# Second mixer's projections: who rounds the weights, and how many PSUM buffers the products have

## Chip, cores and metric

One core of a Trainium2 chip. The metric is the device time of one execution in microseconds (us); before and after are compared by medians of several executions. The profile is one execution taken by the hardware profiler, with times from its first instruction.

## What is computed

A two-layer backbone over 512 latent and 256 context tokens of width 1024. Layer 1 mixes tokens with a bidirectional chunkwise mLSTM; its projections are the stretch in question:

```
p = (t @ w_in).astype(float32)          # t: normalised, modulated tokens (768 x 1024), w_in: 1024 x 3104
q = heads(p[..., :512], 64) * 64 ** -0.5
k = heads(p[..., 512:1024], 64)
v = heads(p[..., 1024:2048], 128)
o = p[..., 2048:3072]                   # later: sigmoid(o), latent tokens only
g = p[..., 3072:3104] + b_gates         # input and forget gates, both directions
```

After it come the mLSTM itself, its output projection, and the mixture of experts of layer 1, whose weights (32 experts) are streamed from HBM.

## The kernel before

Engines: PE = TensorE, ACT = ScalarE, DVE = VectorE, POOL = GpSimd, SP = SyncE, which here issues the loads from HBM.

**Split products.** Matmuls run on a reduced-precision float type (F32R). So each operand is split into a rounded part (hi) and the rest (lo = x - hi), and each product is three matmuls: hi·hi, hi·lo, lo·hi. `Net.split` (L303) does one split: hi on ACT (L306) if no engine is given for it, else with a `tensor_scalar` on that engine (L308); lo with a `tensor_sub` (L309), on POOL for weights. The inner `split` of `ml_in` (L1663) does this for a weight tile of 1024 x 256 in two halves of 128 x 1024 values each; its `eng` is the engine of hi, and None (ACT) by default.

**`ml_in` (L1637).** In a first part, in an order written out by hand (`manual_schedule`, L1709 to 1732), the tokens are transposed and modulated (`norm_T`) for k = 0 to 7, each followed by `chans` (L1688): the products of that k for the gates (PSUM tile psg) and for the first 256 columns of q (psq). Then a loop over i = 0 to 11 takes 256 columns of w_in at a time (i = 0 is done already): i = 1 the second half of q, 2 and 3 k, 4 to 7 v, 8 to 11 o. Each turn loads its weights (L1660, called L(i) below), splits them (split(i)), forms products by `chan` (L1672, 24 matmuls of 512 columns) or by token tile with `toks` (L1680, 24 matmuls of 256 columns), and ACT empties each finished PSUM tile into SBUF (L1769, 1771, 1776, 1782, 1789). A turn of v has six token tiles, a turn of o four.

Between them, turns 1 to 8 do two quarters of the layer's modulation on DVE (`ada_vec`, L194: two loads of 1 MB at L168, then 16 DVE instructions, L202 and L204). Its `finish` comes a turn later, behind the products: tiny matmuls (L210), additions (L214, L218), in some turns a transpose (L227) and a store (L230). `tokens` (L1846) at i = 3 and `ml_queries` (L1879) at i = 9 add some PE and DVE work.

**Buffers.** The pool `ws` has three buffers of 1 MB for L(i) and the ada loads together. `wk` (L1647) has four for each part, so the halves of two turns. `pa` (L1648) has two PSUM tiles of two banks each; a product uses half of one at most. `pb` takes the other four banks. Outside the manual part a scheduler orders each engine's instructions at compile time, by priorities and a cost model, and gives out buffers as it goes; so the order on an engine need not be that of the program, but it is fixed when the kernel runs, and each engine, and SP, works its list in order.

Of the kernel before, what the change touches and what calls it, by code (L numbers as in the profile page):

```python
# [6 lines left out]
F32 = mybir.dt.float32  # L7
# [7 lines left out]
PSUM = bass.MemoryType.PSUM  # L15
ET = mybir.EngineType

P = 128
# [84 lines left out]
class Net:  # L103
# [1533 lines left out]
    def ml_in(self, x, xcp, wsp):  # L1637

        tc, nc, A = self.tc, self.nc, self.A
        V = nc.vector  # L1640
        W = A["l1_ml_w_in"]
        with ExitStack() as st:
            def pool(name, bufs=1, **kw):
                return st.enter_context(tc.tile_pool(name=name, bufs=bufs, **kw))

            hp = pool("h1", side="right")
            wk = pool("i1", 4, side="right")  # L1647
            pa = pool("pa1", 2, space=PSUM)  # L1648
            pb = pool("pb1", 2, space=PSUM)
            hcp = tc.tile_pool(name="h1c", bufs=1, side="right")  # L1650
            hc = hcp.__enter__()
            hs = [[q.tile([P, KD, n], F32R, name=f"h{m}{n}") for m in ("hi", "lo")] for q, n in ((hc, CTX), (hp, SEQ))]
# [5 lines left out]
            def load(c0, n):  # L1658
                w = wsp.tile([P, KD, n], F32, name="ws")
                nc.sync.dma_start(w, W[:, c0:c0 + n].rearrange("(k p) f -> p k f", p=P))  # L1660
                return w

            def split(w, n=256, pool=wk, name="", eng=None, halves=(0, 1)):  # L1663
                parts = []
                for a in halves:
                    hi = pool.tile([P, 4, n], F32R, name=f"{name}whi")
                    lo = pool.tile([P, 4, n], F32R, name=f"{name}wlo")
                    self.split(hi, lo, w[:, 4 * a:4 * a + 4, :], nc.gpsimd, eng)
                    parts.append((hi, lo))
                return parts  # L1670

            def chan(ps, parts, c, t0, t1):  # L1672

                for k in range(KD):
                    (hi, lo), (xh, xl) = parts[k // 4], hk(k, t0, t1)
                    for j, (w, h) in enumerate(((hi, xh), (hi, xl), (lo, xh))):
                        nc.tensor.matmul(ps, w[:, k % 4, c * P:(c + 1) * P], h,
                                         start=k == 0 and j == 0, stop=k == KD - 1 and j == 2)

            def toks(ps, parts, t):  # L1680

                for k in range(KD):
                    (hi, lo), (xh, xl) = parts[k // 4], hk(k, t * P, (t + 1) * P)
                    for j, (w, h) in enumerate(((hi, xh), (hi, xl), (lo, xh))):
                        nc.tensor.matmul(ps, h, w[:, k % 4, :],  # L1685
                                         start=k == 0 and j == 0, stop=k == KD - 1 and j == 2)

            def chans(out, k):  # L1688

                for ps, parts, c, t0, t1 in out:  # L1690
                    (hi, lo), (xh, xl) = parts[k // 4], hk(k, t0, t1)
                    for j, (w, h) in enumerate(((hi, xh), (hi, xl), (lo, xh))):
                        nc.tensor.matmul(ps, w[:, k % 4, c * P:(c + 1) * P], h,
                                         start=k == 0 and j == 0, stop=k == KD - 1 and j == 2)
# [6 lines left out]
            wq0 = load(0, 256)  # L1701
# [6 lines left out]
            wgp = wsp.tile([P, KD, 4, 32], F32, name="ws")  # L1708
            with tc.tile_pool(name="n2", bufs=2, side="right") as wp, tc.manual_schedule(engines={ET.PE, ET.DVE, ET.Activation, ET.Pool}):  # L1709
                nc.gpsimd.memset(wgp, 0.0)  # L1710
                for a in (0, 16):
                    nc.gpsimd.tensor_scalar(wgp[:, :, :, a:a + 8], wg0.rearrange("p k (j h) -> p k j h", h=8),
                                            1.0, 0.0, op0=OP.mult, op1=OP.add)
                parts = split(wgp.rearrange("p k j h -> p k (j h)"), P, wp, "g", nc.gpsimd)
                parts0 = split(wq0, 256, wp, "q", nc.gpsimd)
                turn, modulate = self.norm_T(1, x, self.rs, hs,
                                             lambda: pb.tile([P, 1024], F32, name="pg"), wn)
                psg = pa.tile([P, 1024], F32, name="pa")
                psq = pa.tile([P, 1024], F32, name="pa")
                first = [(psg[:, 512:1024], parts, 0, CTX, NTOK), (psg[:, 256:512], parts, 0, 0, CTX),  # L1720
                         (psq[:, 0:512], parts0, 0, CTX, NTOK), (psq[:, 512:1024], parts0, 1, CTX, NTOK)]
                turn(0)
                turn(1)
                w = load(256, 256)
                parts1 = []
                for k in range(KD):
                    modulate(k)
                    if k + 2 < KD:
                        turn(k + 2)
                    chans(first, k)  # L1730
                    if k in (2, 5):
                        parts1 += split(w, halves=(k // 3,))
# [16 lines left out]
            ps = psg  # L1749
            for q in range(4):  # L1750
                dst = (self.li, self.lf)[q % 2][32 * (q // 2):32 * (q // 2) + 32, :]
                nc.scalar.activation(dst, ps[32 * q:32 * q + 32, 256:1024], AF.Identity, bias=bg[32 * q:32 * q + 32, :])
            tokens = self.ml_gates(sp, gp, pb)

            ada = []
            for i in range(12):
                parts = parts1 if i == 1 else split(load(256 * i, 256)) if i else None
                last, ada = ada, []
                if 1 <= i <= 8:
                    ada = [self.ada_vec(1, 6 + 2 * i + j, wsp, pb, sp, m=1) for j in range(2)]  # L1760
                if i == 0:
                    pass
                elif i < 4:
                    for c in range(2):
                        blk = 2 * (i % 2) + c
                        ps = pa.tile([P, 1024], F32, name="pa")[:, 0:512]
                        chan(ps, parts, c, CTX, NTOK)
                        if i < 2:
                            nc.scalar.activation(self.qT[:, blk, :], ps, AF.Copy, scale=0.125)  # L1769
                        else:  # L1770
                            nc.scalar.activation(self.kT[:, blk, :], ps, AF.Copy)
                    if i >= 2:
                        for t in range(2):
                            ps = pa.tile([P, 1024], F32, name="pa")[:, 0:256]
                            toks(ps, parts, t)
                            nc.scalar.activation(self.kc[:, t, 256 * (i - 2):256 * (i - 1)], ps, AF.Copy)
                elif i < 8:
                    for t in range(NT0):
                        ps = pa.tile([P, 1024], F32, name="pa")[:, 0:256]
                        toks(ps, parts, t)  # L1780
                        h = 2 * (i - 4)
                        nc.scalar.activation(self.v1[:, t, h:h + 2, 0:128],  # L1782
                                             ps.rearrange("p (h e) -> p h e", e=128), AF.Copy)
                else:
                    for t in range(4):
                        ps = pa.tile([P, 1024], F32, name="pa")[:, 0:256]
                        toks(ps, parts, 2 + t)
                        c = slice(256 * (i - 8), 256 * (i - 7))
                        nc.scalar.activation(self.og[:, t, c], ps, AF.Sigmoid)
                if i == 3:  # L1790
                    tokens()
                    gates.__exit__(None, None, None)
                if i == 7:
                    hcp.__exit__(None, None, None)
                if i == 9:
                    self.ml_queries(store.enter_context(tc.tile_pool(name="queries", bufs=1)), pb)
                for f in last:
                    f()
# [371 lines left out]
```

## Time and profile before

| | |
|---|---|
| median of 3 runs | 1930.48 us (1927.62 to 1940.3) |
| the profiled execution | 1943.99 us, span 1942.0 us |
| busy in the span | PE 93%, DVE 49%, ACT 28%, POOL 20% |
| mean granted clock of TensorE | 0.959 |
| `ml_in` from the last products of its first part to the last product | about 1059 to 1263 us |

An answer of the timeline has one line for a group of instructions that follow each other on an engine: start, length of the group, engine, line, operation, output<-input, number; in brackets the idle time in front and what ended it. A length that covers several instructions contains their waits in between. For SP, the start of a line is when the load is issued; it lands later, and the first reader of the data shows when.

### The profile page before, as it was taken

The page shows a single profiled execution, that of the slowest core. Times are in us where ns is not written, and L with a number is a line of the kernel's source. Part 1 is how long each engine was busy: PE and PEld are TensorE (multiplying, and loading weights), DVE is VectorE, ACT ScalarE, POOL GpSimd, SP SyncE. Part 2 cuts the span into 40 slices and gives each one's busy share as a digit, 9 for nine tenths or more (in the row PEclk, how much of TensorE's full clock was granted, in tenths as well). Part 3 has the DMA queues.
Part 4 walks back from the last instruction along what each step waited for, and adds up shares of the span by engine and source line. Part 5 has one row for each costly group of instructions (what it writes and reads, how often), then busy time and mean ns, then how long its engine had stood idle before and what let it go on. Part 6 is the DMA issues. An engine that isn't in the chain of part 4 may idle for free. (4 is left out here: it accounts for less than half of the span.)

```text
span 1942.0 us, 26118 instructions
## 1 busy us (share of the span) xinstructions
PE 1799.0 (93%) x10181; PEld 1009.0 (52%) x10181; DVE 959.3 (49%) x1879; ACT 542.7 (28%) x1007; POOL 387.7 (20%) x300
## 2 busy tenths in 40 slices
PE   7999988897999999999987998999978999999996
PEld 5777775683333333333336898976743333333332
DVE  5577767465454454444455743155552333233334
ACT  5367776222111101111115421145321111111112
POOL 3443311501101000101015242121211111110101
PEclk9999989898999999999998998999988999999998
DMA  9645432547999789999932544200869999999993
GB/s 326 186 142 163 152 109 76 188 152 311 420 419 397 278 326 409 389 403 389 400 117 76 176 139 155 85 1 17 311 257 400 421 421 420 421 422 421 421 420 135
DMA packets 158244, 527.75 MB, mean 272 GB/s; under 512 B 15132, under 2 KB 92194, under 8 KB 109988
## 3 DMA queue, kind: packets, MB, share of 16 engines
q1 hardware_dynamic: 151348, 497.09, 66.5%
q0 software_dynamic: 6768, 28.93, 3.8%
q8 instruction: 82, 1.34, 0.3%
q14 instruction: 46, 0.38, 0.1%
HBM read 518.59 MB, written 7.39 MB: 271 GB/s over the span
## 5 line engine op out<-in xcount | busy, mean ns | idle before, releaser
L1215 DVE TENSOR_TENSOR xl<-xl,ps 128x512 f32<-128x512 f32 x252 | 172.4, 687 | 335.6 <-PE ps L1213 335.6
L1213 PEld LDWEIGHTS ps<-yh,oht 128*128 128x128 f32 x310 | 58.5, 189 | 248.8 <-DVE xl L1215 129.0
L1213 PE MATMUL ps<-yh,oht 128*128 128x512 f32 x310 | 154.1, 497 | 8.9 <-DVEq L1356 6.1
L1200 POOL DMA_INDIRECT xg<-h_rows,idx x32 | 36.7, 1146 | 628.8 <-DVE slot L1185 263.1
L1277 PE MATMUL pd<-wring,hT 128*64 128x512 f32 (+1 forms) x616 | 152.4, 611 | 3.0 <-ACT hT L1269 2.6
L1252 PE MATMUL pu<-wring,xT 128*64 128x512 f32 (+1 forms) x576 | 154.1, 606 | 0.0
L309 POOL TENSOR_TENSOR wlo<-ws,whi 128x1024 fp32r<-128x1024 f32 x41 | 114.8, 2809 | 120.9 <-ACT whi L306 119.4
L1252 PE MATMUL pg<-wring,xT 128*64 128x512 f32 (+1 forms) x576 | 136.9, 601 | 0.0
L1240 POOL TENSOR_TENSOR yl<-yw,yh 128x512 fp32r<-128x512 f32 x60 | 76.6, 1277 | 255.5 <-ACT yh L1239 255.5
L1213 PE MATMUL ps<-yl,oht 128*128 128x512 f32 x310 | 123.5, 398 | 0.0
L1259 ACT ACTIVATE sg<-pg 128x512 f32<-128x512 f32 x32 | 19.1, 597 | 367.6 <-PE pg L1252 367.6
L1685 PE MATMUL pa<-whi,hhi 128*128 128x256 f32 x352 | 104.3, 296 | 9.1 <-ACT v L1782 9.0
L1239 ACT ACTIVATE yh<-yw 128x512 fp32r<-128x512 f32 x64 | 40.3, 630 | 251.7 <-DVE yw L1236 127.9
L1231 DVE SCALAR_TENSOR_TENSOR yw<-pd,slotr,gt2b 128x512 f32<-128x512 f32 x62 | 46.5, 751 | 118.9 <-PE pd L1277 118.9
L1685 PE MATMUL pa<-whi,hlo 128*128 128x256 f32 x352 | 103.3, 293 | 0.0
L1685 PE MATMUL pa<-wlo,hhi 128*128 128x256 f32 x352 | 102.9, 292 | 0.0
L1252 PE MATMUL pu<-yt,xT 128*64 128x512 f32 (+1 forms) x408 | 101.7, 605 | 0.0
L1208 ACT ACTIVATE xT<-tr 128x512 f32<-128x512 f32 x64 | 35.1, 596 | 221.0 <-PE tr L1207 221.0
L1277 PE MATMUL pd<-yt,hT 128*64 128x512 f32 (+1 forms) x376 | 87.6, 599 | 1.5 <-ACT hT L1269 1.0
L1252 PE MATMUL pg<-yt,xT 128*64 128x512 f32 (+1 forms) x400 | 84.7, 599 | 0.0
L1215 DVE TENSOR_TENSOR xc<-xc,ps 128x512 f32<-128x512 f32 x64 | 43.7, 687 | 82.1 <-PE ps L1213 82.0
L1277 PEld LDWEIGHTS pd<-wring,hT 128*64 128x64 f32 (+1 forms) x616 | 44.3, 133 | 75.7 <-issue 69.6
(627 smaller groups left out, 3727.9 us busy)
## 6 DMA issues: line engine op xcount, KB each, us to landing
wring<-in_l_moe_w_gate_dram SPq DMA_DIRECT2D x62, 1024.0 KB
wring<-in_l_moe_w_up_dram SPq DMA_DIRECT2D x61, 1024.0 KB
wring<-in_l_moe_w_down_dram SPq DMA_DIRECT2D x59, 1024.0 KB
yt<-in_l_moe_w_up_dram SPq DMA_DIRECT2D x41, 1024.0 KB
ws<-in_l_ada_w_dram SPq DMA_DIRECT2D x40, 1024.0 KB
yt<-in_l_moe_w_gate_dram SPq DMA_DIRECT2D x39, 1024.0 KB
yt<-in_l_moe_w_down_dram SPq DMA_DIRECT2D x35, 1024.0 KB
ws<-in_l_moe_w_gate_dram SPq DMA_DIRECT2D x24, 1024.0 KB
```

Source lines behind the costliest of these rows:

```text
L309: eng_lo.tensor_sub(lo, x, hi.bitcast(F32))
L1200: nc.gpsimd.indirect_dma_start(out=xg, out_offset=None, in_=hd, in_offset=bass.IndirectOffsetOnAxis(ap=idx[:, 0:1], axis=0))
L1208: nc.scalar.activation(xT[:, 4 * h:4 * h + 4, :], pt[:, :, 0:n], AF.Copy)
L1213: nc.tensor.matmul(ps, lhsT, y, start=i == 0, stop=i == len(ys) - 1)
L1215: V.tensor_add(xs, xs, ps)
L1231: V.scalar_tensor_tensor(y[k], ps, r[:, 1:2], g[:, 0, :], op0=OP.mult, op1=OP.mult)
L1239: nc.scalar.activation(yh, y, AF.Copy)
L1240: eng.tensor_sub(yl, y, yh.bitcast(F32))
L1252: nc.tensor.matmul(ps[a:a + w, :], xT[:, 4 * h + j, a:a + w], pieces[n, e[i], h][:, j, :], start=h == 0 and j == 0, stop=h == 1 and j == 3)
L1259: nc.scalar.activation(s, pg, AF.Silu)
L1277: nc.tensor.matmul(pd[a:a + w, :], hT[:, 2 * h + j, a:a + w], ring.down(2 * p + i, h, j, c), start=h == 0 and j == 0, stop=h == 1 and j == 1)
L1685: nc.tensor.matmul(ps, h, w[:, k % 4, :], start=k == 0 and j == 0, stop=k == KD - 1 and j == 2)
```

## The change

The inner `split` rounds on GpSimd by default, so ACT has no weight split left in `ml_in`; POOL does hi and lo one after the other. The two large PSUM tiles of the first part move into a pool of their own, `pa0`, which is closed before the loop; the loop gets a pool of four single-bank tiles in the same four banks.

```
-            pa = pool("pa1", 2, space=PSUM)
             pb = pool("pb1", 2, space=PSUM)
+            pa0 = tc.tile_pool(name="pa0", bufs=2, space=PSUM)
+            pa = pa0.__enter__()
...
-            def split(w, n=256, pool=wk, name="", eng=None, halves=(0, 1)):
+            def split(w, n=256, pool=wk, name="", eng=nc.gpsimd, halves=(0, 1)):
...
-                parts = split(wgp.rearrange("p k j h -> p k (j h)"), P, wp, "g", nc.gpsimd)
-                parts0 = split(wq0, 256, wp, "q", nc.gpsimd)
+                parts = split(wgp.rearrange("p k j h -> p k (j h)"), P, wp, "g")
+                parts0 = split(wq0, 256, wp, "q")
...
             tokens = self.ml_gates(sp, gp, pb)
+            pa0.__exit__(None, None, None)
+            pa = pool("pa1", 4, space=PSUM)
...
-                        ps = pa.tile([P, 1024], F32, name="pa")[:, 0:512]
+                        ps = pa.tile([P, 512], F32, name="pa")
...
-                            ps = pa.tile([P, 1024], F32, name="pa")[:, 0:256]
+                            ps = pa.tile([P, 512], F32, name="pa")[:, 0:256]
```

The last edit is made at all three places where `toks` gets its PSUM tile (L1774, 1779, 1786).

## Rows read from the trace of the kernel before

**Rows 1.** Busy us of PE, PEld, DVE, ACT, POOL (instructions); clock, DMA share, GB/s.
```profile
1116.00:1263.00 147.00, 133.91 (x1024) 130.17 (x1023) 50.34 (x118) 29.64 (x54) 43.10 (x14) 0.93 0.40 127
...
1500.00:1600.00 100.00, 98.31 (x458) 35.40 (x456) 31.39 (x62) 12.59 (x26) 14.35 (x11) 1.00 1.01 421
```

**Rows 2.** What SP waited for, whole span: total us, times, longest.
```profile
SPq L93 <- DVE keys L2008: 119.6, 1, 119.6
```

**Rows 3.** Timeline of PE, turns i = 5, 7, 8 and 9.
```profile
1134.68 0.36 PE L1685 MATMUL pa<-whi,hhi 128*128 128x256 f32 x1
1141.71 0.39 PE L1685 MATMUL pa<-whi,hhi 128*128 128x256 f32 x1 [3.92 <-ACT v L1782]
1146.18 0.28 PE L1685 MATMUL pa<-whi,hhi 128*128 128x256 f32 x1
...
1149.06 0.28 PE L1685 MATMUL pa<-whi,hhi 128*128 128x256 f32 x1
...
1176.77 0.36 PE L1685 MATMUL pa<-whi,hhi 128*128 128x256 f32 x1
1190.21 0.28 PE L1685 MATMUL pa<-whi,hhi 128*128 128x256 f32 x1
...
1202.53 0.36 PE L1685 MATMUL pa<-whi,hhi 128*128 128x256 f32 x1
1209.75 0.41 PE L1685 MATMUL pa<-whi,hhi 128*128 128x256 f32 x1
...
1219.57 0.36 PE L1685 MATMUL pa<-whi,hhi 128*128 128x256 f32 x1
```

**Rows 4.** Timeline of ACT, the hi halves of split(4), split(6) and split(8).
```profile
1102.55 2.01 ACT L306 ACTIVATE whi<-ws 128x1024 fp32r<-128x1024 f32 x2 [5.46 <-DMA ws<-in_l_ml_w_in_dram]
...
1139.38 2.00 ACT L306 ACTIVATE whi<-ws 128x1024 fp32r<-128x1024 f32 x2 [7.80 <-DMA ws<-in_l_ml_w_in_dram]
...
1182.66 2.00 ACT L306 ACTIVATE whi<-ws 128x1024 fp32r<-128x1024 f32 x2 [8.99 <-DMA ws<-in_l_ml_w_in_dram]
```

**Rows 5.** Timeline of SP, the loads into `ws`.
```profile
1090.00 0.99 SPq L168 DMA_DIRECT2D ws<-in_l_ada_w_dram  x2
1097.15 0.37 SPq L1660 DMA_DIRECT2D ws<-in_l_ml_w_in_dram  x1
...
1128.08 1.01 SPq L168 DMA_DIRECT2D ws<-in_l_ada_w_dram  x2
...
1169.83 0.99 SPq L168 DMA_DIRECT2D ws<-in_l_ada_w_dram  x2
```

**Rows 6.** Timeline of POOL, the lo halves of split(5) and split(7).
```profile
1120.36 7.69 POOL L309 TENSOR_TENSOR wlo<-ws,whi 128x1024 fp32r<-128x1024 f32 x2 [10.32 <-ACT whi L306]
...
1159.53 10.27 POOL L309 TENSOR_TENSOR wlo<-ws,whi 128x1024 fp32r<-128x1024 f32 x2 [12.71 <-ACT whi L306]
```

**Rows 7.** Durations of the split's instructions: ns min/median/max, first and last start.
```profile
L306 ACT ACTIVATE whi<-ws x22: 1040/1058/1115, 1037.0 to 1231.3; 128x1024 fp32r<-128x1024 f32 x22
L309 POOL TENSOR_TENSOR wlo<-ws,whi x22: 2332/2400/7920, 1040.2 to 1233.3; 128x1024 fp32r<-128x1024 f32 x22
...
L308 POOL TENSOR_SCALAR whi<-ws x19: 1041/1054/2485, 22.4 to 293.0; 128x1024 fp32r<-128x1024 f32 x19
```

**Rows 8.** Timeline of ACT and PE from the first part into the loop.
```profile
1059.09 1.06 ACT L306 ACTIVATE whi<-ws 128x1024 fp32r<-128x1024 f32 x1 [2.93 <-DMA ws<-in_l_ml_w_in_dram]
1060.05 0.40 ACT L306 ACTIVATE hhi<-hf 128x256 fp32r<-128x256 f32 x1
...
1063.50 0.89 ACT L1752 ACTIVATE li<-pa,bg 32x768 f32<-32x768 f32 x1 [2.10 <-PE pa L1693]
...
1065.56 1.08 ACT L1748 ACTIVATE qT<-pa 128x512 f32<-128x512 f32 x2 [0.27 <-PE pa L1693]
...
1062.90 0.39 PE L1693 MATMUL pa<-hlo,gwhi 128*128 128x256 f32 x1 [2.02 <-DVE hlo L309]
...
1066.70 0.79 PE L1677 MATMUL pa<-hhi,whi 128*128 128x512 f32 x1 [1.17 <-ACT qT L1748]
```

More of the change, by code (lines that the diff above doesn't have):

```diff
@@ L1778, in ml_in @@
                     for t in range(NT0):
-                        ps = pa.tile([P, 1024], F32, name="pa")[:, 0:256]
+                        ps = pa.tile([P, 512], F32, name="pa")[:, 0:256]
                         toks(ps, parts, t)
@@ L1785, in ml_in @@
                     for t in range(4):
-                        ps = pa.tile([P, 1024], F32, name="pa")[:, 0:256]
+                        ps = pa.tile([P, 512], F32, name="pa")[:, 0:256]
                         toks(ps, parts, 2 + t)
```

## The prediction, made before the changed kernel ran

> **What bounds the kernel now.** I read the busy time in windows first. In the loop of `ml_in`, PE is busy for 133.9 of 147 us, while ACT, POOL and DVE are busy for 29.6, 43.1 and 50.3 [rows 1]. So PE is the bound, and the mean granted clock of 0.93 says that some of the rest is time after a pause, at the lower of the two levels. What can be won here is PE's pauses with what follows them, nothing else. The next question is whether a gain here reaches the end. The first expert load of layer 1 waits 119.6 us on SP for the last work of the attention that follows `ml_in` [rows 2], and once it runs the DMA engines are full (share 1.01 and 421 GB/s from 1500 to 1600 us [rows 1]). The stream is long and begins when the attention ends: what `ml_in` saves moves the whole stream forward, one for one.
>
> Then the timeline of PE. One undisturbed token tile takes 2.88 us (1146.18 to 1149.06). At the start of turn 5 two tiles take 11.50 us instead of 5.76, and at the start of turn 7 13.44 (1176.77 to 1190.21); the row at 1141.71 names the releaser, an emptying copy on ACT [rows 3]. The timeline of ACT shows why it was late: in ACT's list the hi copies of a later turn's weights stand in front of the emptying copies of a tile that is done, and they wait 7.8 and 9.0 us for a load to land [rows 4]. With two PSUM tiles PE can go on for one tile, then it stands. After the pause the second tile still takes 4.47 us (1141.71 to 1146.18), which is the lower clock.
>
> **The change, part by part.**
>
> *ACT loses the weight splits.* Twenty-two copies of 1.06 us [rows 7] leave ACT; their 23 us are worth nothing as such, as ACT has time. What counts is that an emptying copy no longer stands behind a DMA wait. That takes away 11.50 - 5.76 = 5.7 us in turn 5 and 13.44 - 5.76 = 7.7 us in turn 7. In turn 8 one tile takes 7.22 us (1202.53 to 1209.75 [rows 3]), 4.3 too many; no ACT copy of weights ended that pause, so I credit between 0 and 4.3.
>
> *The seam before the loop.* At 1059.09 ACT waits 2.93 us for the weights of turn 2, and the last hi of the tokens (1060.05) comes behind that; PE then waits 2.0 us for the lo made from it [rows 8]. Without the weight copy that hi runs at once, and PE's last products come about 3 us earlier.
>
> *Four single banks.* ACT is busy for a fifth of the loop [rows 1], so two tiles suffice once it is free; four only add cover. But the loop's first tiles now lie where `pa0` lay. Before, the first product of the loop (1066.70) waited only for the copies of q. Now its bank is that of the gates' tile, and I take it that all of that tile's copies must be done: 4 x 0.89 + 1.08 = 4.6 us [rows 8] from about 1060.4, so 1065.0. Of the 3 us earlier, 1.7 remain. Bounds: 0, if closing the pool waits for more, and 3.4, if it waits for no more than before.
>
> *POOL gets the hi copies.* On POOL one costs 1.05 us, as in the layer-0 code where POOL makes them, against 1.06 on ACT; a lo costs 2.40 [rows 7]. Before, a split took 1.06 + 2 x 2.40 = 5.9 us from landing to end, since the second hi ran beside the first lo; now 2 x (1.05 + 2.40) + 0.1 of gaps = 7.0. Each split is 1.1 us longer. Behind it stands a chain. SP's pair of ada loads is issued the moment split(5) ends (1120.36 + 7.69 = 1128.05 [rows 6], 1128.08 [rows 5]), and likewise at 1169.83 behind split(7) (1159.53 + 10.27): their buffer is the one that the split read. L(i+1) stands behind them. It lands 11.3 us later (1128.08 to 1139.38) or 12.8 (1169.83 to 1182.66) [rows 4, 5]; I take 12.0. So the period of the chain is 12.0 + 7.0 + c, where c is what POOL loses to DVE.
>
> *c.* Two lo's took 7.69 and 10.27 us where 4.8 is undisturbed [rows 6, 7]: 2.9 and 5.5 lost, both while DVE worked on `ada_vec`. c lies between 0 and 5.5 per turn. As PE no longer falls behind, DVE's work, which starts when a turn's products end, falls mostly into the 12 us in which POOL waits for the load, so I take 1.0.
>
> The rule that speaks against the change is in the Trainium skill, SBUF — State Buffer, section "Who interferes with whom": a DVE instruction with two SBUF inputs and a GpSimd instruction that reads SBUF exclude each other for the whole instruction, whichever comes first. The trace agrees (a lo of 7.92 us, a hi of 2.49 on POOL [rows 7]). Taken as holding in every turn, it is the third rival below.
>
> *The sum.* From the third tile of turn 5 to the start of turn 7 (1149.06 to 1176.77 [rows 3]) PE does nine tiles and twice the small products between turns: (27.71 - 9 x 2.88) / 2 = 0.9 us each. So PE needs 6 x 2.88 + 0.9 = 18.2 us for a turn of v; the chain gives 12.0 + 7.0 + 1.0 = 20.0. split(4) and split(5) are each 1.1 longer, so split(5) ends at 1128.05 + 2.2 = 1130.3, still in time for turn 5 on PE (1134.68 - 1.7 = 1133.0). Then split(6), (7), (8), (9) end at 1150.3, 1170.3, 1190.3 and 1210.3. PE would want them at 1151.2, 1169.4, 1188.5 and, after a turn of o (4 x 2.88 + 0.9 = 12.4), 1202.7. So the pauses that ACT caused go, and a new one of nearly 8 us comes at turn 9, whose predecessor is shorter than the chain. Turn 9 starts at 1210.3 instead of 1219.57 [rows 3]: 9.3 us earlier. After the pause one tile runs at the lower clock, 4.47 - 2.88 = 1.6 us. From there on nothing is won or lost: no ada loads come after turn 8, a load alone takes 5.4 us (1097.15 to 1102.55 [rows 4, 5]), and 5.4 + 7.0 = 12.4 is about a turn of o. `ml_queries` stays as it was. Gain 9.3 - 1.6 = 7.7 us.
>
> The profiled execution took 1943.99 us, 13.5 more than the median of 1930.48; nothing in this stretch depends on that, so I take the 7.7 us off the median: 1922.8.
>
> **The rivals.**
>
> *PE stays the bound (faster).* The scheduler gives out buffers at compile time. At 1090.00 the ada pair was issued 7 us ahead of L(4) [rows 5], into buffers that DVE had freed. If the longer splits make it choose so in every turn, L(i+1) comes alone: 5.4 + 7.0 + 1.0 = 13.4 us, far less than 18.2. Then nothing is given back: 1.7 + 5.7 + 7.7 = 15.1, and between 0 and 4.3 of turn 8, say 17.3 us: 1913.2 (1911.1 to 1915.4). Against it: from turn 5 on the pair waited for POOL.
>
> *The lock takes the gain (slower).* With c = 5.5 in each of the four turns the period is 24.5, split(9) ends at 1130.3 + 98.0 = 1228.3, 8.7 us later than turn 9 starts now, and with the clock's 1.6 the time is 1940.8. It turns into a loss from a period of (1219.57 - 1.6 - 1130.3) / 4 = 21.9, so from c = 2.9. For it: split(5) and split(7) lost 2.9 and 5.5, and POOL's share of the turn grows by a third. Against it: DVE's burst comes once a turn, and mostly in POOL's wait for the load.
>
> *Nothing arrives.* The pauses go, but other work behind them (tokens, the queries, the copies at the attention's start) keeps its time: 1930.5. Against it: PE names no other releaser of that size in the loop, and the stream waits for the attention's end [rows 2].
>
> **How the numbers follow.** Chances: the forecast 0.50, PE stays the bound 0.28, the lock 0.12, nothing arrives 0.10. I predict the likeliest, 1922.8 us. The range is 1910 to 1935: it holds the forecast with its own bounds (0 to 3.4 at the seam, c from 0 to 2.9), nearly all of the first rival and the third, and leaves out the lock at its full price. By itself the likeliest case reaches from 1916 to 1931. About 1% (19.3 us) is what a measurement can tell from no change; so faster means under 1911.2 and slower over 1949.8. Faster takes the first rival at its upper end with more won in turn 8 or at the seam: 0.13. Slower needs the lock and a further loss, such as a worse order given out by the scheduler: 0.05. Within 1%: 0.82.
>
> **What the profile after would show.** Right: no wait of PE for an ACT copy at the starts of turns 5 and 7; hi copies on POOL at about 1.05 us; the ada pairs issued at the end of a split; a pause of PE in front of turn 9 that POOL's lo ends; the loop's first product at about 1065. Wrong: ada pairs ahead of the splits (the first rival), POOL pairs above 12 us in every turn (the lock), or a later first product, if closing the pool costs more than the copies. A different order of PE's own list, which four banks allow, would also upset the sum.

## The result, and the profile after

The changed kernel takes 1941.0 us (median of 20 runs, 1934.6 to 1977.8), the kernel before in the same runs 1936.1. Their ratio is 1.0053 [1.0029, 1.0078]: the change costs about 10 us (5.6 to 15) where 7.7 were to be won. The profiled execution has a span of 1936.3 us. Some executions of any of these kernels run for long parts at a lower TensorE clock and are left out of the ratios; four profiled executions of that kind (the fourth of the kernel before, the second of the changed one, late_act's and the second of late_act_load) are used here for single stretches alone.

The same 147 us of the loop, shifted by 3 us, as this execution is 3.35 us earlier (columns as in [rows 1]):

```profile
1113.00:1260.00 147.00, 133.01 (x1042) 128.72 (x1042) 51.40 (x121) 17.76 (x43) 61.70 (x30) 0.93 0.43 137
```

ACT has lost 12 of its 29.6 us and POOL has gained 18.6, as the change says. PE's busy time and its clock (0.93) are what they were [rows 1]. The waits of PE show why: none of them is on an emptying copy of `v` any more, and others stand in their place (1013 to 1232 us: total us, times, longest).

```profile
PE pg L227 <- DVE modT L218: 8.6, 1, 8.6
...
PE pa L1678 <- ACT lf L1753: 3.5, 1, 3.5
PE pa L1686 <- POOL wlo L309: 2.7, 2, 1.8
PE pa L1694 <- POOL hlo L288: 2.5, 1, 2.5
PE pg L1894 <- DVE sel L1893: 2.4, 3, 1.2
```

They sum to 19.7 us. In the same stretch of the kernel before the waits, counted the same way (without L272, 6.3 us there and 5.3 here), sum to 17.2: 9.0 on `v` and 2.9 on L218 in the loop, 4.1 at the seam [rows 3, 8], 1.2 on `sel`. The timeline of PE shows where the new ones lie, at the seam and in turn 8:

```profile
1056.21 0.50 PE L1694 MATMUL pa<-hlo,gwhi 128*128 128x512 f32 x1 [2.46 <-POOL hlo L288]
...
1064.66 0.60 PE L1678 MATMUL pa<-hhi,whi 128*128 128x512 f32 x1 [3.46 <-ACT lf L1753]
...
1188.85 0.36 PE L1686 MATMUL pa<-whi,hhi 128*128 128x256 f32 x1
...
1199.74 0.38 PE L227 MATMUL pg<-ident,modT 128*8 128x128 f32 x1 [8.61 <-DVE modT L218]
...
1213.56 0.36 PE L1686 MATMUL pa<-whi,hhi 128*128 128x256 f32 x1
```

Turn 8 begins at 1188.85 and turn 9 at 1213.56, 24.7 us for four tiles that need 12.4: of the rest 8.6 are this wait and 0.9 one for lo, and some 2.8 come from the lower clock after it (0.72 granted on the mean of this turn).

**The splits.** On the timeline of POOL the first hi half of each split should take 1.05 us:

```profile
1140.12 3.75 POOL L308 TENSOR_SCALAR whi<-ws 128x1024 fp32r<-128x1024 f32 x1 [11.70 <-DMA ws<-in_l_ml_w_in_dram]
...
1147.45 2.39 POOL L309 TENSOR_TENSOR wlo<-ws,whi 128x1024 fp32r<-128x1024 f32 x1
1162.44 3.95 POOL L308 TENSOR_SCALAR whi<-ws 128x1024 fp32r<-128x1024 f32 x1 [12.61 <-DMA ws<-in_l_ml_w_in_dram]
...
1183.80 3.98 POOL L308 TENSOR_SCALAR whi<-ws 128x1024 fp32r<-128x1024 f32 x1 [11.50 <-DMA ws<-in_l_ml_w_in_dram]
...
1205.33 3.53 POOL L308 TENSOR_SCALAR whi<-ws 128x1024 fp32r<-128x1024 f32 x1 [11.68 <-DMA ws<-in_l_ml_w_in_dram]
```

It takes 3.5 to 4.0 in all four turns; the rest of the split is undisturbed. DVE's timeline shows what ran beside it (its list in turns 6 and 8):

```profile
1137.06 0.35 DVE L202 TENSOR_SCALAR vpart<-ws,cT 128x256 f32<-128x256 f32 x1 [2.66 <-DMA ws<-in_l_ada_w_dram]
1137.32 5.63 DVE L204 SCALAR_TENSOR_TENSOR vpart<-ws,cT,vpart 128x256 f32<-128x256 f32 x14
...
1189.11 1.13 DVE L218 TENSOR_TENSOR modT<-modT,svm 128x2 f32<-128x2 f32 x1
1199.26 0.35 DVE L202 TENSOR_SCALAR vpart<-ws,cT 128x256 f32<-128x256 f32 x1 [9.02 <-DMA ws<-in_l_ada_w_dram]
1199.53 0.15 DVE L218 TENSOR_TENSOR modT<-modT,svm 128x2 f32<-128x2 f32 x1
```

The burst of 14 two-input instructions begins when the second ada load lands, at 1137.3, and ends at 1142.95. L(6) comes next on SP's queue and lands 2.8 us after the burst began, so POOL's hi stands until the burst is nearly over: 1142.95 + 1.05 is close to its end at 1143.87. In turn 9 it ends 0.3 us before the burst does (1208.86 and 1209.14). The three loads come in a fixed order, and in turns 6 to 9 of all three executions of this kernel the burst has a lead of 2.6 to 2.8 us and hi takes 3.5 to 4.0.

The last two rows are the second wait. The list of DVE has, in turn 8, one L218, then the L202 of the next ada vector, then the other L218. The L202 waits 9.0 us for its load, which SP issued when split(8) ended:

```profile
1128.44 1.01 SPq L168 DMA_DIRECT2D ws<-in_l_ada_w_dram  x2
...
1193.68 0.99 SPq L168 DMA_DIRECT2D ws<-in_l_ada_w_dram  x2
```

PE's transpose stands for the L218 behind it. The head of ACT's list that waited for a load is gone; the head of DVE's list took its place. It hides another wait: the first product of turn 9 that needs the second lo of split(9) begins at 1215.31, only 0.45 us after that lo ends (1205.33 + 9.53 = 1214.86). Without the wait on L218, PE would have stood for the split instead.

### The profile page after: what moved, and what is told of

Read it like the earlier page. It is cut to its first block, busy times and chain, and to the rows that moved or that the text cites. A ratio compares the mean times of both kernels' runs of the same rounds, so it can differ in the third digit from the quotient of the medians.

```text
span 1936.3 us, 26120 instructions
## 1 busy us (share of the span) xinstructions
PE 1792.7 (93%) x10181; PEld 1007.0 (52%) x10181; DVE 960.3 (50%) x1879; ACT 522.2 (27%) x985; POOL 412.8 (21%) x322
## 5 line engine op out<-in xcount | busy, mean ns | idle before, releaser
L308 POOL TENSOR_SCALAR whi<-ws 128x1024 fp32r<-128x1024 f32 x41 | 64.8, 1582 | 230.5 <-DMA ws<-in_l_ml_w_in_dram 95.6
L309 POOL TENSOR_TENSOR wlo<-ws,whi 128x1024 fp32r<-128x1024 f32 x41 | 103.2, 2521 | 2.8
```

The costliest lines, as they stand in the source:

```text
L308: eng_hi.tensor_scalar(hi, x, 1.0, 0.0, op0=OP.mult, op1=OP.add)
L309: eng_lo.tensor_sub(lo, x, hi.bitcast(F32))
```

## The experiments

The stretch named below runs from the first hi of the gates' weights on POOL (1018.16 us in the kernel before) to the first product of the last token tile. It was 242.0 us in the kernel before and 240.3 after.

| kernel | median us | ratio to before | stretch, us |
|---|---|---|---|
| before, profiled four times | 1930.5 to 1942.9, by set of runs | 1 | 242.0, 240.7, 239.0, 228.4 |
| changed, profiled three times | 1941.0 | 1.0053 [1.0029, 1.0078] | 240.3, 239.9, 243.9 |
| psum_only | 1932.3 | 0.9978 [0.9936, 1.0020] | 233.6 |
| pool_only (4 runs) | 1952.9 | 1.0101 [1.0031, 1.0171] | 235.6 |
| no_burst | 1926.6 | 0.9947 [0.9913, 0.9980] | 225.9 |
| f_first | 1933.1 | 1.0001 [0.9968, 1.0034] | 237.7 |
| load_first | 1941.4 | 1.0035 [0.9992, 1.0077] | 235.2 |
| both_pool | 1945.2 | 1.0069 [1.0038, 1.0101] | 247.9 |
| both_act | 1934.6 | 1.0031 [0.9990, 1.0073] | 238.1 |
| late_act (6 runs) | 1951.5 | not compared | 228.5 |
| late_pool | 1934.8 | 1.0011 [0.9983, 1.0039] | 239.7 |
| seam_act | 1936.4 | 1.0028 [0.9990, 1.0067] | 244.0 |
| late_act_load, twice | 1928.0 and 1949.7 | 0.9973 [0.9941, 1.0006] and 1.0030 [0.9989, 1.0072] | 229.3, 233.0 |
| late_pool_load | 1936.7 | 1.0011 [0.9990, 1.0032] | 239.0 |

**The kernel before again (b_again).**

> The kernel before, unchanged, a second time, for its profile. Its profiled execution took 1943.99 us, its median over twenty runs 1936.1. Theory A (the changed kernel's new waits cost what the old ones did): the waits of ScalarE for a load, in front of finished tiles, vary from execution to execution with the landing of the loads, and in a typical execution PE loses less than the 13.4 us of the first profile to them (5.7 in turn 5, 7.7 in turn 7); then this profile shows another split of these waits, with a sum between 0 and 13 us. Theory B (the first profile is typical): the two pauses come again within 1 us, and the loss of the changed kernel lies outside this loop.

The pauses on `v` sum to 9.1 us against 9.0, the one on L218 to 3.1 against 2.9. The two pauses came again, as Theory B says, in this second execution.

**Each half of the change alone.** psum_only takes the four single banks and leaves hi on ACT; pool_only takes one default and leaves the two double tiles:

```diff
-            def split(w, n=256, pool=wk, name="", eng=None, halves=(0, 1)):
+            def split(w, n=256, pool=wk, name="", eng=nc.gpsimd, halves=(0, 1)):
```

> The changed kernel with the hi copies back on ScalarE; the four single banks stay. Theory A: the cost sits in the longer splits on GpSimd, so without them the chain of loads is as before; ScalarE still waits for loads in front of finished tiles, but four tiles let PE go on for three more tiles (8.6 us) instead of one, so pauses of 4 to 5 us at turns 5 and 7 go: 6 to 14 us faster than before, 12 to 22 faster than the changed kernel. Theory B: the new pool at the seam or a worse order by four banks costs; then this kernel is as slow as the changed one, 1941, or slower than before by 5 or more.

> The kernel before with the hi copies on GpSimd alone; two tiles of two banks as before. Theory A: within 4 us of the changed kernel (1937 to 1945), as ScalarE free of waits needs no third tile, with the same chain: splits from landing to end of 8.5 to 10 us, a period of about 21.5 us, PE waiting in turns 8 and 9. Theory B (the banks are the cost): 5 to 10 us faster than the changed kernel.

PE's waits in psum_only and in pool_only:

```profile
PE pa L1686 <- ACT v L1785: 1.6, 2, 1.4
```

```profile
PE pg L227 <- DVE modT L218: 7.5, 1, 7.5
```

Four banks alone nearly end the waits on `v`, 9.0 us down to 1.6, with ACT's list as it was: PE runs ahead through the free banks while ACT waits for its load. The prediction gave the banks no worth of their own ("four only add cover"). The hi part on GpSimd alone brings the wait on L218 with it, as in the changed kernel. So the wait on L218 comes with GpSimd's part. In time, psum_only can't be told from the kernel before, but its interval lies below the changed kernel's (its Theory A wanted 6 to 14 us). pool_only missed the 1937 to 1945 us expected of it by 8, though its stretch, 235.6, is shorter than three of the four of the kernel before; its time rests on four runs whose mean clock was 0.947 to 0.957, against 0.961 in the first profile of the changed kernel, so it says little of the hi part.

**Without DVE's burst.** 14 of the 16 instructions that make one turn's `vpart` are left out, so the modulation of this kernel is not the reference's.

```diff
-            for k in range(1, KD):
+            for k in range(1, KD if m == 2 else 1):
```

> The changed kernel with 14 of the 16 VectorE instructions of each turn's modulation left out (only the first of eight terms of each dot product is formed), the loads as they are. Theory A: the splits on GpSimd are no longer held up by VectorE's burst, so each takes 7.0 us instead of 8.7 to 10, the period falls from 21.5 to 18.5 to 19 us, split(9) ends about 10 us earlier, and the time falls by 6 to 12 us against the changed kernel. Theory C (the lock costs nothing, since PE waits for loads or for VectorE's queue anyway): within 2 us of the changed kernel.

The split of turn 6 on POOL's timeline, first and last instruction:

```profile
1129.60 1.05 POOL L308 TENSOR_SCALAR whi<-ws 128x1024 fp32r<-128x1024 f32 x1 [12.82 <-PE pa L1686]
...
1134.24 2.40 POOL L309 TENSOR_TENSOR wlo<-ws,whi 128x1024 fp32r<-128x1024 f32 x1
```

Now hi takes its 1.05 us, the split 7.04, and POOL waits for PE to free a buffer, not for a load. TensorE is the bound, a turn takes 18.2 us, and the stretch is 14 us shorter. This is the first rival of the prediction, in a kernel without the burst: it is the burst that keeps it away. Whether it does so through the split alone this run can't part, since DVE's own list is shorter too, and the wait on L218 falls to 1.6 us.

**Repairing the two waits.** f_first puts the previous turn's L210, L214, L218 and L227 ahead of this turn's ada loads, so that no L218 stands behind an L202 that waits. load_first loads L(i+1) ahead of the ada pair. both_pool does both, both_act does both with hi on ACT.

```diff
 # f_first
                 last, ada = ada, []
+                for f in last:
+                    f()
 ...
-                for f in last:
-                    f()
 # load_first
-                parts = parts1 if i == 1 else split(load(256 * i, 256)) if i else None
+                parts = parts1 if i == 1 else split(nxt) if i else None
+                if 2 <= i < 11:
+                    nxt = load(256 * (i + 1), 256)
```

> The changed kernel, with the last step of each turn's modulation chain (VectorE's L218 and TensorE's transpose of it) put ahead of the next turn's two modulation loads in program order, so that L218 no longer stands behind an L202 that waits for a load. Nothing is left out. Theory A (the wait moved into two places: VectorE's list, where L218 stood behind such an L202 for 8.6 us in turn 8, and the period of load and split, 21 to 22 us instead of 20): the wait of the transpose L227 falls from 8.6 to under 2 us, but turn 9 still can't begin its lo products before the ninth split ends, so only 0 to 4 us are gained against the changed kernel. Theory C (VectorE's list alone carries the loss): the whole 8.6 us come back, and the time is 7 to 9 us below the changed kernel. Theory D (the loop is not what separates the two kernels): within 2 us of the changed kernel.

> The changed kernel, with the load of the next 256 columns issued right behind each split, ahead of the two modulation loads instead of behind them. Nothing is left out. Theory A (the period of 12 us for three loads, 7 us for the split and 2.8 us for VectorE's burst on it sets the pace of turns 5 to 9): one load of about 4 to 6 us instead of three stands in the chain, the period falls under TensorE's own 18 us a turn, the splits end before their products want them, and the loop is 5 to 12 us shorter than in the changed kernel; the wait of L227 behind VectorE's L202 may stay, at up to 8 us in one turn. Theory C (VectorE's list alone): the wait of L227 stays or grows, since the modulation loads now land later, and no more than 2 us are gained. Theory D: within 2 us of the changed kernel.

> The changed kernel with both reorderings at once: the load of the next columns ahead of the two modulation loads, and L218 with its transpose ahead of VectorE's wait for them. Nothing is left out. Theory A: both new waits go, TensorE works through the loop at 18 to 19 us a turn, and the loop is 8 to 14 us shorter than in the changed kernel, so that this kernel is about 4 to 10 us below the kernel before. Theory C: no better than the first reordering alone. Theory D: within 2 us of the changed kernel.

> The kernel before (hi part on ScalarE) with the four single banks of the change and with both reorderings. Nothing is left out. Theory A: with the load early, ScalarE's hi part no longer waits for a load in the middle of emptying PSUM, so the pauses of 5 to 8 us of the kernel before go without moving the hi part to GpSimd; the split is 5.9 us, VectorE's burst stretches only its lo part; no hlo wait in the first part; loop 10 to 15 us shorter than in the kernel before, 3 us or more below the other reordered kernel. Rival: ScalarE still has 3.7 us more to do in each turn than in the changed kernel, and waits for PSUM of 2 to 5 us a turn stay; then it is at or above the reordered kernel with both parts on GpSimd.

From turn 5 to the last tile these four need 109.2, 109.3, 109.3 and 108.7 us, against 123.0 in the changed kernel and 125.5 before. But in turns 1 to 4 DVE works on the gates, and reordered steps wait for it (f_first, then both_pool):

```profile
PE pg L227 <- DVE modT L214: 6.9, 1, 6.9
```

```profile
PE pg L210 <- DVE vpart L204: 6.7, 1, 6.7
PE pg L1857 <- DVE sT L1859: 5.8, 1, 5.8
```

Turn 5 begins 117.3 us into the stretch in the changed kernel, and 128.5, 125.9, 138.5 and 129.4 in these. What the late turns gained the early ones gave back; for both_pool more than that. And as PE came 9 to 21 us later to turn 5, the loads had that much more time: these runs don't show that a repair made the late turns short. The totals of Theory A were missed.

**The repairs from turn 5 on only.** late_act and late_pool move the steps of f_first in turns 5 to 9 alone, with hi on ACT and on GpSimd, both with four banks. late_act_load and late_pool_load add the early load from turn 5 on.

```diff
+                if i >= 5:
+                    for f in last:
+                        f()
 ...
-                for f in last:
-                    f()
+                if i < 5:
+                    for f in last:
+                        f()
```

> The kernel before (hi part on ScalarE) with the four single banks, and with L218 and its transpose ahead of the next modulation loads in turns 5 to 9 only, where VectorE has nothing else to do; in turns 1 to 4, in which VectorE works on the gates, the order stays that of the kernel before (the reordering of all turns had cost 10 us there in the earlier runs). Nothing is left out. Theory A (the two waits in the loop, VectorE's list and the period of the splits, make the loss; moving hi to GpSimd only adds to it): turn 5 begins about 118 us after the first GpSimd product, as in the kernel with four banks alone, and the rest takes 109 to 112 us instead of 115.7; 1926 to 1931 us, 2 to 6 us below the kernel before. Theory D (what happens in the loop is given back later, or the loop of an unprofiled run of the kernel before is already that short): no faster than the four banks alone.

> As the previous kernel, and from turn 5 on the next columns are loaded ahead of the two modulation loads. Nothing is left out. Theory A: if the period of load and split still binds in turns 6 to 9, another 1 to 4 us go; if TensorE already binds there, nothing changes within 1 us. A loss would mean that the modulation's steps, now later, are waited for.

> The changed kernel with L218 and its transpose ahead of the next modulation loads in turns 5 to 9 only. Nothing is left out. Theory A: turns 1 to 4 as in the changed kernel (turn 5 begins 117 us after the first GpSimd product), turns 5 to the end about 109 to 116 us instead of 123, so 5 to 10 us less than the changed kernel, about level with the kernel before. Theory C (VectorE's list is a minor part, the period of the splits binds): no more than 3 us less. Theory D: within 2 us of the changed kernel.

> The changed kernel (both weight parts on GpSimd, four single banks) with L218 ahead of the next modulation loads and the next columns loaded ahead of them, from turn 5 on. It differs from late_act_load in the engine of the hi part alone. Nothing is left out. If the waits behind the split's period and VectorE's list made the loss, and GpSimd's hi costs nothing once its load comes early: the stretch from the first GpSimd product to the last token tile is 226 to 231 us as in late_act_load (229.3), and the time is within 2 us of it. If hi on GpSimd costs by itself (the split of 7 to 10 us against 5 to 6): stretch of 233 us or more, and 3 us or more slower than late_act_load.

> late_act_load again, beside its partner with hi on GpSimd, on the same chip: 228 to 231 us for the stretch, and 0.1 to 0.6% below the kernel before.

late_act has no comparison in time; its stretch is 228.5 us, at a granted clock of 0.96. Here turn 5 begins when it does in the changed kernel (117.5 to 119.0 us into the stretch), and the late turns can be compared. Three pairs differ in the engine of hi alone, in us from turn 5 to the last tile:

| order of the list | hi on ACT | hi on GpSimd |
|---|---|---|
| as in the changed kernel | 115.7 (psum_only) | 123.0 (changed) |
| L218 early from turn 5 | 110.4 (late_act) | 122.2 (late_pool) |
| L218 and load early from turn 5 | 110.9, 114.0 (late_act_load, twice) | 121.6 (late_pool_load) |

With GpSimd neither repair helps, and 7 to 12 us separate the pairs. These numbers contain turn 10, which takes 16.2 us at a granted clock of 1.00 and 25.0 at 0.66 (psum_only); from turn 5 to turn 9 alone the pairs are 69.2 and 81.5, 73.3 and 82.2, and 73.7 or 76.8 against 83.3. The times of executions with a mean clock of 0.96 or more go the same way: 1925.8 to 1936.2 us (psum_only) and 1934.6 to 1942.5 (changed) for the first pair, 1922.4 to 1930.4 and 1925.1 to 1929.2 (late_act_load, twice) and 1933.3 to 1938.8 (late_pool_load) for the third. So Theory A, by which the order of the two lists made the loss, falls: what is left is the engine of hi. That it acts through the longer time that POOL holds what it shares with DVE is read from the timelines, not tested by itself. The timelines of late_pool_load (POOL, DVE, DVE) and its wait of PE are:

```profile
1176.84 1.10 POOL L308 TENSOR_SCALAR whi<-ws 128x1024 fp32r<-128x1024 f32 x1 [10.87 <-PE pa L1686]
...
1176.94 9.51 DVE L204 SCALAR_TENSOR_TENSOR vpart<-ws,cT,vpart 128x256 f32<-128x256 f32 x8
...
1186.55 0.23 DVE L218 TENSOR_TENSOR modT<-modT,svm 128x2 f32<-128x2 f32 x2
```

```profile
PE pg L227 <- DVE modT L218: 7.0, 1, 7.0
```

Here POOL came first, by 0.1 us. Its split ran at full speed, DVE's eight instructions took 9.5 us instead of some 3.2 (14 take 5.63), and L218 behind them came late. In late_pool the same happens to two bursts in a row, held up by two splits, and PE waits 11.1 us for an L218. Whichever engine gives way, PE waits for it: for lo, or for L218. With hi on ACT, POOL's part of the split is 4.8 us instead of 7, and PE's waits on DVE in the two executions of late_act_load are 3.6 and 6.5 us against 10.5.

No version that does all the work is faster than the kernel before beyond doubt: late_act_load showed 0.9973 and 1.0030, and both intervals hold 1. The second time it missed what was expected of it, in the stretch (233.0) and in the ratio.

**Is one execution typical?** The stretch of the two first profiles differed by 1.7 us in favour of the changed kernel, while the times differ by 10 us the other way. (The first expectation below compares runs at one TensorE clock: within a kernel the span grows by some 1.8 us for each 0.001 that its mean clock is lower, as from 1920.3 us at 0.966 to 1968.8 at 0.940 in runs of the kernel before.)

> The kernel before, unchanged, profiled a third time. What this tells: its unprofiled runs, put at one TensorE clock, are some 3 to 4 us faster than its two profiled executions say, and those of the changed kernel are not. Theory E (the pauses of 5 to 8 us behind ScalarE's list come in some executions and not in others): this execution may show a loop that is 5 us or more shorter than the 241 us of the other two. Theory F (the pauses come in every execution, and what varies lies outside the loop): 240 to 243 us again.

> The kernel before, profiled a fourth time. The first three showed 242.0, 240.7 and 239.0 us for the stretch. Theory E: this one may lie below 239; theory F: 239 to 242.

> The changed kernel, unchanged, profiled a second time. If its waits behind GpSimd's split and VectorE's L218 differ between executions (theory E), the stretch from the first GpSimd product to the last token tile is 243 us or more here, against 240.3 in the first profile, and the waits in turns 6 to 9 sum to more than the 12 us of the first; if they are the same in every execution (theory F), 239 to 241.5 us, and the loss lies elsewhere.

> The changed kernel, profiled a third time. As the second: over 243 us by theory E in at least one of the two, 239 to 241.5 us in both by theory F.

The changed kernel keeps to its pattern: 8.6, 8.6 and 8.3 us on L218 in three executions, and turn 9 begins 197.0 to 198.8 us into the stretch. The 243.9 us of the third come from turn 10: 25.3 us at a granted clock of 0.73, against 20.6 at 0.83 in the first. The kernel before does not keep to its own. Its fourth profile has no wait on L218 and a single one on `v`, and its stretch is 228.4 us. The lo halves of split(7) and split(8) and DVE's bursts tell why, in that execution:

```profile
1155.63 4.95 POOL L309 TENSOR_TENSOR wlo<-ws,whi 128x1024 fp32r<-128x1024 f32 x2 [12.43 <-PE pg L227]
1174.79 5.24 POOL L309 TENSOR_TENSOR wlo<-ws,whi 128x1024 fp32r<-128x1024 f32 x2 [14.21 <-ACT whi L306]
...
1155.84 9.79 DVE L204 SCALAR_TENSOR_TENSOR vpart<-ws,cT,vpart 128x256 f32<-128x256 f32 x14
...
1173.95 9.92 DVE L204 SCALAR_TENSOR_TENSOR vpart<-ws,cT,vpart 128x256 f32<-128x256 f32 x14
```

In the first profile of before, the lo halves took 10.27 us [rows 6] and the burst 5.61:

```profile
1159.58 5.61 DVE L204 SCALAR_TENSOR_TENSOR vpart<-ws,cT,vpart 128x256 f32<-128x256 f32 x14
```

In turn 7 both begin within 0.2 us of each other, in either execution, POOL first by the record, and one time DVE pays and the other time POOL. In turn 8 of the fourth execution DVE even has a lead of 0.84 us and pays. When DVE pays, the split ends 5.3 us sooner, the next loads go out sooner, and the pause of turn 7 does not come. In the changed kernel the burst has a lead of 2.6 to 2.8 us, and POOL pays each time.

**The seam.** Only the hi halves of the split made inside the first part go back to ACT.

```diff
-                        parts1 += split(w, halves=(k // 3,))
+                        parts1 += split(w, eng=None, halves=(k // 3,))
```

> The changed kernel with the hi halves of the second split (the one made inside the first part, between the products over k) back on ScalarE; everything in the loop as in the changed kernel. Nothing is left out. If GpSimd's hi part ahead of the first norm's lo part (2.5 us of TensorE waiting at that place in the changed kernel's trace) makes the loss: 2 to 4 us less than the changed kernel. By the theory of the loop: the wait goes or becomes one behind ScalarE of about the 2 to 3 us that the kernel before shows there, and the time is within 1.5 us of the changed kernel's.

In the changed kernel POOL's list had a hi half, itself waiting for its load, ahead of the tokens' lo:

```profile
1053.27 1.49 POOL L308 TENSOR_SCALAR whi<-ws 128x1024 fp32r<-128x1024 f32 x1 [5.32 <-DMA ws<-in_l_ml_w_in_dram]
1054.73 2.11 POOL L288 TENSOR_TENSOR hlo<-hf,hhi 128x512 fp32r<-128x512 f32 x2
```

In seam_act no wait for a lo is left in the first part, and the loop's first product comes 46.7 us into the stretch, against 49.9 in the changed kernel and 48.5 before. The ratio, 1.0028 against 1.0053, points to some 5 us, but the intervals overlap. The stretch of its one profile was no shorter: turn 9 begins 0.9 us earlier than in the changed kernel, and turn 10 took 25.1 us at a granted clock of 0.66.

## Why the prediction was wrong, step by step

- **ACT's pauses in turns 5 and 7.** Right: the waits on `v` went. But the banks alone would have done it (1.6 us left), so the engine that made hi did not have to change for it.
- **The undisturbed split, 7.0 us, and the loads, 12.0.** Right: 7.04 without the burst, and 11.8 on the mean of the four turns (11.68, 12.57, 11.47, 11.65). The ada pair was issued at the split's end in every turn, so the first rival did not come.
- **c, the step that failed.** I took 1.0, with the reason that DVE's burst "falls mostly into the 12 us in which POOL waits for the load". The four splits took 9.72, 9.86, 9.86 and 9.53 us, so c is 2.5 to 2.9, 2.7 on the mean. The burst starts when an ada load lands, and that is 2.6 to 2.8 us before the load that POOL waits for; SP's queue ties the two together. That DVE's work starts when a turn's products end was wrong. Four turns at 1.7 more are 6.8 of the 9.3 us of turn 9: it began 198.8 us into the stretch, against 201.4 before and 192.1 as forecast. With 2.7 for c the same sum gives a gain of 9.3 - 6.8 - 1.6 = 0.9 us. The trace of before hinted at it: its two bad splits lost 2.9 and 5.5. The rule that I weighed, from the Trainium skill, SBUF — State Buffer, "Who interferes with whom", held here: the hi with one input stands for 2.5 to 2.9 us behind DVE's instructions with two. The Trainium skill says there, too, that the order of issue decides who blocks. Here the recorded order does not settle it: in turn 9 of the changed kernel POOL's hi, begun at 1205.33, stood while instructions of the burst that began after it ran at full speed, and in the fourth profile of before a lo that began 0.84 us into the burst lost under 0.5 us. (In the prediction this rule's case is the second of the rivals, the lock, not the third.)
- **A wait that no step named.** The prediction followed the late split to the next load and to lo, not to DVE: split(8) late, ada load late, L202 late, the L218 in DVE's list behind it late, PE late by 8.6 us. The wait on L218 stood at 2.9 us in the kernel before, in the part of turn 8 that I credited with 0 to 4.3 us of gain. It grew instead. It hardly adds to c, though: it stands where the forecast had its pause of nearly 8 us, and without it turn 9 could have used its second lo 0.45 us sooner, no more (an estimate from 1215.31 and 1214.86). In the third profile PE waits for that lo as well, 0.44 us.
- **The seam.** The bank rule was right, since PE waits for `lf` for 3.5 us, and a gain of 1.7 us is about what seam_act shows (1.9). But the change gave POOL the hi that ACT had had in front of the tokens' work, and POOL makes the tokens' lo. So the same head-of-list wait moved to POOL, and the loop began 1.3 us later than before, a miss of 3.0. It is no term of the sum: the chain of splits sets turn 9, which seam_act, 3.2 us earlier into the loop, reached 0.9 us earlier.
- **The lock as the losing rival.** Its break-even at c = 2.9 was nearly met, and I had given it 0.12. It takes the gain, and at 2.7 it makes no loss by itself: turn 9 began 2.6 us earlier than before, and the stretch of the first profiles is 1.7 us shorter. The three pairs show what hi on GpSimd costs against hi on ACT when both have four banks: 7 to 12 us from turn 5 on.
- **The base of the forecast.** "Nothing in this stretch depends on that", I wrote of the profiled execution, which took 13.5 us more than the median. The stretch does vary: 242.0, 240.7, 239.0 and 228.4 us in four executions of the kernel before, and the pauses were read from the longest. The median of 1930.48 us, too, came from three runs; twenty gave 1936.1. The time came out 18.2 us above the forecast: 5.6 are this base, 7.7 the gain that did not come, and 4.9 a loss, by the medians (10 by the ratio). The chance of 0.82 for a time within 1% of the kernel before came true, but with a loss in place of the gain.
- **What of the loss is open.** Over twelve kernels of the table (without pool_only and its four runs) the median span goes by about 0.8 us for each us of the stretch (225.9 to 247.9), within 5 us. The kernels' mean stretches, 237.5 before and 241.4 after, then make some 3 of the 10 us. Put at one clock of 0.962 by the 1.8 us above, the executions with a mean clock of 0.955 or more have a median span of 1932 us before and 1936 after: 4 us, about as much. The execution of before in which DVE gives way is in that mean as one of four, and its attention behind `ml_in` ran at a granted clock of 0.71; how often such executions come in the timed runs was not found. The remaining part of the loss is not settled by these runs. It need not be in the loop.

## What to carry to other kernels

Moving an instruction that waits for a load from one engine's list to another moves the wait with it: look at what stands behind it in the new list, and at the producer that this list feeds. Where an engine that shares SBUF access gets work that starts on a load, ask what the other engine starts on the load before it in the same queue, since a fixed order of loads can make the collision come every time, as it did here in twelve turns of three executions. Try first, alone, the part of a change that only adds buffers; here it removed the waits that the other part was meant to remove.

## What was not expected of the hardware

- Two instruction streams that start within 0.2 us of each other (POOL's lo and DVE's burst) were served either way: 10.27 and 5.61 us in one execution, 4.95 and 9.79 in another. A burst that had begun 0.84 us ahead gave way too (9.92, with the lo at 5.24). The length of the stretch went with it: 242.0 us and 228.4.
- TensorE's clock fell to its lower level (1.2 GHz) while PE was, by the profile, busy all the time. The same stretch of the attention, with the same list, in the first and the second profile of before (windows, columns as in [rows 1]):

```profile
1300.00:1360.00 60.00, 60.00 (x324) 41.66 (x321) 35.99 (x110) 35.74 (x130) 6.95 (x11) 1.00 0.05 18
```

```profile
1300.00:1360.00 60.00, 60.00 (x266) 40.76 (x266) 31.66 (x96) 26.82 (x101) 6.52 (x10) 0.80 0.01 2
```

  In the second the granted clock was 1.00 up to 1334 us and 0.50 from 1338 to 1358. From the last token tile to the first expert load it took 95.7 us with the first and 104.4 with the second. This came in kernels of every kind (0.83 in pool_only, 0.80 in no_burst, 1.00 in psum_only and in the changed kernel), and what decides it was not found.
